# First projections of a hybrid trunk: groups of two, two, six and six k tiles, k tiles 2 to 5 modulated in pairs

## The chip, the cores and the metric

The kernel runs on one core of a Trainium2 chip. The metric is the time of one execution on the device in microseconds (us), as the median of the runs; less is better. The core has five engines that run side by side and meet by semaphores: TensorE (PE; its weight loads are shown as PEld), VectorE (DVE), ScalarE (ACT), GpSimd (POOL) and SyncE (SP), which here issues the transfers between HBM and the core's memory. Each engine takes its own list of instructions in order.

## The reference

One layer of a hybrid trunk, on x of 512 x 2048 and one conditioning vector c of 2048, all in float32. What matters here is its beginning:

```python
mod = c @ w_ada[l] + b_ada[l]
sh1, sc1, g1, sh2, sc2, g2 = [m[:, None, :] for m in jnp.split(mod, 6, axis=-1)]
h = x * (1.0 + sc1) + sh1
mix = token_mixer(h, ...)        # begins with proj = h @ w_in
x = layer_norm(ALPHA * x + g1 * mix, ln1_g[l], ln1_b[l])
h = x * (1.0 + sc2) + sh2
ff = jnp.square(jax.nn.relu(h @ w_ff1[l])) @ w_ff2[l]
x = layer_norm(ALPHA * x + g2 * ff, ln2_g[l], ln2_b[l])
```

`proj` is split into u, the convolution's inputs, q, k, v, and the indexer's qi, ki and wi. No column of `h` is known before its scale and shift are, and these need a product of c with 16 x 256 weights for each 128 columns.

## The kernel before

**Tiles.** The 2048 columns of `h` are 16 k tiles of 128. `acts` holds them transposed, 128 columns x 512 tokens, each as a high and a low half: `split(h, l, src)` has ACT round to fp32r (`wh` of a weight, L57) and DVE subtract (`wl` of a weight, L60). A product of two float32 numbers is three matmuls (`mm3`, `mm3n`): high x high, low x high, high x low.

**Modulation of w k tiles (`start_k`).** DVE accumulates c[i] times 16 blocks of w_ada into the tile `adaz` of 128 x 256w (`ada_acc`: one instruction a block on L63, the first of a tile on L67; loads `raw`, four buffers of 1 MB). PE adds up its 128 partitions against `ones` (L299, tile `sc`). DVE adds the bias and one (tile `mod`). Then, for each of the w k tiles, ACT forms `hf` = x * scale + shift (x comes as the tile `xk`), ACT rounds it into `acts`, and DVE subtracts for its low half. Two buffers each hold `adaz`, `xk` and `hf`.

**First projections.** u and kiwi (weights `wA` and `wkw`), then qi (`wqi`, two halves), then q (`wq`, two halves) are computed in four groups of k tiles, `KGROUPS`. A group does all five weight blocks for its k tiles. A k tile costs 15 matmuls for `wA` and `wkw`, 2 x 9 for `wqi` and 2 x 12 for `wq`: 57, nearly all with 512 columns. The weights of two k tiles come as one tile `rw`, and are split as one piece of 128 x 1024. At the end of a group its sums leave PSUM (`evac_acc`): by ACT in the first group, by DVE, which adds them to what is there (`u_t`, `qi_n`, `q_t`), in the others. Two banks of u and that of kiwi stay in PSUM through all groups.

**Order.** Work is written group by group; the accumulations for the next group's k tiles are written a step at a time between this group's weights (`pace`, `tick`), and `ensure(k1 - 1)` writes out what is still missing of a group's k tiles ahead of its first weights. A scheduler with priorities (`PRIO`) then sets the order on each engine; on the chip each engine follows that order. The groups are called 0 to 3 below.

Of the kernel before, what the change touches and what calls it, by code (L numbers as in the profile page):

```python
# [16 lines left out]
SEQ, D, NT, KT = 512, 2048, 4, 16  # L17
# [2 lines left out]
NH, HD = 8, 128  # L20
IH = 16
TOPK = 128
KGROUPS = ((0, 2), (2, 6), (6, 10), (10, 16))

PRIO = dict(cols=40000, ada_bias=4000, mod=4000, kw=4000, first=4000, evac=1000, values=300, att=600, mixer=150,
            wo=5000, ln1=150, ff1=3000, ff2=4000, hc=300, hc_load=300, tx=2000, ln2=150, index=-100, topk=60, rope=600, ssm0=600, ssm=300, glu=150,
# [25 lines left out]
def trunk_kernel(ctx, tc, A, out):  # L52
# [3 lines left out]
    def act(o, i, f=AF.Copy, **kw):  # L56
        S.activation(o, i, f, **kw)  # L57

    def tt(o, a, b, op):
        V.tensor_tensor(o, a, b, op=op)  # L60
# [4 lines left out]
    def ts(o, a, s1, s2, op0, op1=None):  # L65
        if op1 is None:
            V.tensor_scalar(o, a, s1, None, op0=op0)  # L67
        else:
            V.tensor_scalar(o, a, s1, s2, op0=op0, op1=op1)
# [11 lines left out]
    def prio(name):  # L81
        if name not in PRIO:
            name += str(stage_no[0])
        return tc.high_priority(offset=PRIO[name])

    def bank(n="mm"):
        if "two" in pools:
            return two_banks()[:, 0]
        return pools[n].tile([128, 512], F32, name=n)
# [9 lines left out]
    def col(n, i=0, w=1):  # L99
        o = COLS[n][0]  # L100
        return cols[:, o + i:o + i + w]
# [18 lines left out]
    def split(h, l, src):  # L120
        act(h, src)
        tt(l, src, h.bitcast(F32), OP.subtract)
# [92 lines left out]
    def ada_acc(srcs, n, brow=None, ways=1, pool=None):  # L215


        z = (pool or AZ[0]).tile([128, ways * n], F32, name="adaz", bufs=2 if pool else 1)
        if brow is not None:
            G.memset(z, 0.0)  # L220
            with prio("ada_bias"):
                nc.sync.dma_start(z[0:1, :], brow)
        i = 0
        for s in srcs:
            r = load(s, [128, s.shape[1], n], *ada_raw, prio_="ada_load")
            with prio("ada"):
                for j in range(s.shape[1]):
                    o = z[:, (i % ways) * n:(i % ways + 1) * n]
                    if i < ways and brow is None:
                        ts(o, r[:, j], col("c", i), None, OP.mult)  # L230
                    else:
                        stt(o, r[:, j], col("c", i), o, OP.mult, OP.add)
                    i += 1
            yield z

    def ada_block(blk, sink, row=False):
        src = [A["adaR"][blk][:, 2 * j:2 * j + 2] for j in range(8)]
        for z in ada_acc(src, 1024, A["bR"][blk:blk + 1, :] if row else None):
            yield
        sink(z)  # L240
# [9 lines left out]
    def to_cols(dst, bias):  # L250
        def sink(z):
            ps = bank("sc")
            for j in range(8):
                T.matmul(ps[:, j:j + 1], z[:, j * 128:(j + 1) * 128], ones[:, 0:1], start=True, stop=True)
            tt(dst, ps[:, 0:8], bias, OP.add)
        return sink
# [25 lines left out]
    def start_k(k, w):  # L282

        if w == 4:
            src = A["adaS4"][(k - 2) // 4]
        else:
            src = A["adaS2"][k // 14][:, :, 256 * (k % 2):256 * (k % 2 + w)]
        step = 8 // w
        ways = 2 if w == 1 else 1
        for i, z in enumerate(ada_acc([src[:, a:a + step] for a in range(0, 16, step)], 256 * w,  # L290
                                      ways=ways, pool=FP)):
            if i < 2 * w - 1:
                yield
        ps = bank("sc")
        mod = FP.tile([128, 2 * w], F32, name="mod")
        for j in range(2 * w):
            for a in range(ways):
                c0 = (a * 2 * w + j) * 128
                T.matmul(ps[:, j:j + 1], z[:, c0:c0 + 128], ones[:, 0:1], start=a == 0, stop=a == ways - 1)  # L299
        with prio("mod"):  # L300
            tt(mod, ps[:, 0:2 * w], col("bS", 2 * k, 2 * w), OP.add)
            sc_ = mod.rearrange("p (k two) -> p k two", two=2)[:, :, 0]
            ts(sc_, sc_, 1.0, None, OP.add)
            for j in range(w):
                xk = FP.tile([128, SEQ], F32, name="xk")
                nc.sync.dma_start(xk, A["xT"][k + j])
                hf = FP.tile([128, SEQ], F32, name="hf")
                act(hf, xk, AF.Identity, scale=mod[:, 2 * j:2 * j + 1], bias=mod[:, 2 * j + 1:2 * j + 2])
                split(acts[:, k + j, 0], acts[:, k + j, 1], hf)
        ready[0] = k + w  # L310
        yield

    def start_all():
        k = 0
        while k < KT:
            w = 1 if k < 2 else min(4, KT - k)
            yield from start_k(k, w)
            k += w

    bg.append(start_all())  # L320

    held = [bank("sa"), bank("sa"), bank("sb")]

    def ensure(k):
        while ready[0] <= k:
            tick()
# [4 lines left out]
    for j in range(2):  # L331
        mod_jobs.append(ada_block(2 + j, to_cols(mod2[:, 1, 8 * j:8 * j + 8], col("b2", 8 * j, 8))))
        mod_jobs.append(ada_block(4 + j, to_cols(mod2[:, 0, 8 * j:8 * j + 8], col("b2", 16 + 8 * j, 8))))
    for gi, (k0, k1) in enumerate(KGROUPS):
        n_ada = 2 * (KGROUPS[gi + 1][1] - KGROUPS[gi + 1][0]) if gi + 1 < len(KGROUPS) else PUMP["start"]
        n_w = 5 * (k1 - k0) - (k1 - k0 if gi == 0 else 0)
# [8 lines left out]
        if gi > 0:  # L345
            ensure(k1 - 1)
        if gi == len(KGROUPS) - 1:
            bg.extend(mod_jobs[:3])
# [686 lines left out]
    with prio("ln1"):  # L1035
        for t in range(NT):
# [3 lines left out]
            for kq in range(4):  # L1040
                ps = bank(("sa", "sb")[kq % 2])
                for j in range(4):
                    k = 4 * kq + j
                    T.transpose(ps[:, j * 128:(j + 1) * 128], r1[:, t, k * 128:(k + 1) * 128], ident)
                hf = WO.tile([128, 4, 128], F32, name="hf2", bufs=3)
                for j in range(4):
                    k = 4 * kq + j
# [582 lines left out]
```

## Time and profile before

| | |
|---|---|
| median of 3 runs | 2221.06 us (2219.15 to 2222.51) |
| the profiled execution | 2218.12 us |
| its span from first to last instruction | 2216.3 us |
| PE busy | 2138.7 us, 96% of the span |
| DVE busy | 1878.6 us, 85% |
| ACT busy | 1041.5 us, 47% |

The first projections are the first 250 us of the span. All rows are of the profiled execution; its span is 1.8 us shorter than its time. A busy PE is not always a PE at its peak: matmuls overlap each other, so that a wait of less than about 0.2 us between two of them does not show as idle time, and the distance from start to start is the better measure.

### The profile page before, as it was taken

What the parts mean: (1) busy time and instruction counts of PE and PEld (TensorE: products, weight loads), DVE (VectorE), ACT (ScalarE), POOL (GpSimd) and SP (SyncE); (2) the same over time, 40 slices, a digit from 0 to 9 for tenths busy, and PEclk for the clock granted to TensorE, in tenths of its full rate; (3) what the DMA queues carried; (4) which work ended last, traced back from release to release, by engine and by line L of the source; (5) the groups of instructions that cost most, each with busy time, mean ns of one, the idle gap of its engine ahead of it and who ended that gap; (6) DMA issues with size and microseconds to landing.
All of it is one profiled execution on the core that took longest, in us unless ns stands there. A gap on an engine that the chain in (4) does not pass through costs nothing.

```text
span 2216.3 us, 30985 instructions
## 1 busy us (share of the span) xinstructions
PE 2138.7 (96%) x12043; PEld 1845.9 (83%) x12043; DVE 1878.6 (85%) x2520; ACT 1041.5 (47%) x1394; POOL 44.6 (2%) x55
## 2 busy tenths in 40 slices
PE   6999999998999999989999999999899999999997
PEld 4778887876777787889999999999778887888886
DVE  7886799999867776798888888886789988998788
ACT  3423444344644313666666665665444444444432
POOL 0000000010000000000000000000000000000000
PEclk9999999999999999999999999999999999999999
DMA  8887653364334676756566556564888898798462
GB/s 326 316 305 280 200 216 135 107 235 164 103 119 157 243 277 255 241 172 229 182 205 203 188 198 206 181 209 141 301 295 275 280 318 280 245 341 275 134 218 86
DMA packets 198171, 489.80 MB, mean 221 GB/s; under 512 B 18052, under 2 KB 106500, under 8 KB 171656
## 3 DMA queue, kind: packets, MB, share of 16 engines
q1 hardware_dynamic: 191496, 475.24, 61.0%
q0 software_dynamic: 6528, 12.58, 3.1%
q8 instruction: 94, 1.54, 0.3%
q14 instruction: 53, 0.43, 0.1%
HBM read 394.45 MB, written 80.74 MB: 214 GB/s over the span
## 4 chain that ended last, share of the span: by engine, by line
PE 50%; issue 29%; DVE 14%; DMA 4%; ACT 3%; SPq 0%; POOL 0%; DVEq 0%; ACTq 0%; POOLq 0%
PE two L1396 7%; PE two L1397 7%; PE two L1395 7%; PE mm L209 4%; PE mm L197 4%; PE mm L210 4%; PE mm L208 3%; PE mm L198 3%; PE mm L196 3%; DVE wl L60 3%; DVE adaz L63 2%; PE two L210 1%; PE two L209 1%; PE two L208 1%; DVE x L60 1%
## 5 line engine op out<-in xcount | busy, mean ns | idle before, releaser
L57 ACT ACTIVATE wh<-raw 128x1024 fp32r<-128x1024 f32 x332 | 351.1, 1058 | 437.5 <-PE two L1397 140.8
L60 DVE TENSOR_TENSOR wl<-raw,wh 128x1024 fp32r<-128x1024 f32 x332 | 403.7, 1220 | 106.5 <-ACT wh L57 105.3
L1395 PE MATMUL two<-wh,hin 128*128 128x512 f32 x784 | 307.4, 392 | 5.7 <-ACT wh L57 5.0
L1396 PE MATMUL two<-wl,hin 128*128 128x512 f32 x784 | 306.5, 391 | 4.1 <-DVE wl L60 4.0
L1397 PE MATMUL two<-wh,hin 128*128 128x512 f32 x784 | 305.8, 390 | 0.0
L196 PE MATMUL mm<-acts,wh 128*128 128x512 f32 (+1 forms) x568 | 223.0, 396 | 5.7 <-ACT wh L57 3.3
L197 PE MATMUL mm<-acts,wl 128*128 128x512 f32 (+1 forms) x568 | 224.0, 394 | 1.7 <-DVE wl L60 1.5
L198 PE MATMUL mm<-acts,wh 128*128 128x512 f32 (+1 forms) x568 | 221.2, 391 | 0.0
L63 DVE SCALAR_TENSOR_TENSOR adaz<-raw,cols,adaz 128x1024 f32<-128x1024 f32 (+2 forms) x180 | 198.2, 1111 | 16.9 <-DMA raw<-in_adaR_dram 12.8
L202 PE MATMUL mm<-acts,wh 128*128 128x256 f32 x720 | 204.0, 283 | 3.1 <-ACT wh L57 2.4
L203 PE MATMUL mm<-acts,wl 128*128 128x256 f32 x720 | 203.8, 283 | 1.8 <-DVE wl L60 1.8
L203 PE MATMUL mm<-tx,wl 128*128 128x256 f32 x720 | 203.8, 283 | 1.1 <-DVE wl L60 1.1
L204 PE MATMUL mm<-acts,wh 128*128 128x256 f32 x720 | 203.7, 283 | 0.0
L204 PE MATMUL mm<-tx,wh 128*128 128x256 f32 x720 | 203.3, 282 | 0.0
L202 PE MATMUL mm<-tx,wh 128*128 128x256 f32 x720 | 202.0, 281 | 0.1
L1395 PEld LDWEIGHTS two<-wh,hin 128*128 128x128 f32 x784 | 147.7, 188 | 38.0 <-ACT wh L57 6.2
L1396 PEld LDWEIGHTS two<-wl,hin 128*128 128x128 f32 x784 | 147.6, 188 | 37.9 <-DVE wl L60 6.6
L209 PE MATMUL mm<-wl,acts 128*128 128x512 f32 x448 | 175.1, 391 | 1.7 <-DVE wl L60 1.5
L210 PE MATMUL mm<-wh,acts 128*128 128x512 f32 x448 | 174.5, 390 | 0.0
L208 PE MATMUL mm<-wh,acts 128*128 128x512 f32 x448 | 173.6, 391 | 0.2 <-DVE r L60 0.2
L1397 PEld LDWEIGHTS two<-wh,hin 128*128 128x128 f32 x784 | 147.6, 188 | 30.7
L57 ACT ACTIVATE wh<-st 128x1024 fp32r<-128x1024 f32 x90 | 95.5, 1061 | 105.3 <-PE mm L204 82.8
(316 smaller groups left out, 4514.5 us busy)
## 6 DMA issues: line engine op xcount, KB each, us to landing
raw<-in_wff_dram SPq DMA_DIRECT2D x232, 512.0 KB, 4.9
hc_d<-hc SPq DMA_DIRECT2D x98, 512.0 KB, 5.1
hin<-hc_d SPq DMA_DIRECT2D x49, 1024.0 KB, 9.2
raw<-in_adaR_dram SPq DMA_DIRECT2D x48, 1024.0 KB, 5.6
raw<-in_adaS_dram SPq DMA_DIRECT2D x32, 1024.0 KB, 9.0
raw<-in_wo_dram SPq DMA_DIRECT2D x16, 1024.0 KB, 5.3
araw<-in_adaR_dram SPq DMA_DIRECT2D x16, 1024.0 KB, 7.8
raw<-in_wconv_dram SPq DMA_DIRECT2D x12, 1024.0 KB, 5.0
```

The lines of the kernel that those rows point to most:

```text
L57: S.activation(o, i, f, **kw)
L60: V.tensor_tensor(o, a, b, op=op)
L196: T.matmul(ps, wh, xh, start=start, stop=False)
L197: T.matmul(ps, wl, xh, start=False, stop=False)
L198: T.matmul(ps, wh, xl, start=False, stop=stop)
L202: T.matmul(ps, wh, xh, start=start, stop=False, skip_group_check=True)
L203: T.matmul(ps, wl, xh, start=False, stop=False, skip_group_check=True)
L204: T.matmul(ps, wh, xl, start=False, stop=stop, skip_group_check=True)
L209: T.matmul(ps, xh, wl, start=False, stop=False)
L1395: T.matmul(ps[:, t], xh, h[:, k], start=first, stop=False, skip_group_check=True)
L1396: T.matmul(ps[:, t], xh, l[:, k], start=False, stop=False, skip_group_check=True)
L1397: T.matmul(ps[:, t], xl, h[:, k], start=False, stop=last, skip_group_check=True)
```

## The change

The four groups become k tiles 0-1, 2-3, 4-9 and 10-15, where they were 0-1, 2-5, 6-9 and 10-15. K tiles 2-3 and 4-5 are modulated as two pairs (w = 2), where they were one group of four (w = 4); k tiles 6-9 and 10-13 stay groups of four, 14-15 a pair. For a pair the source is half of each block of four in HBM, in runs of 2 KB.

```diff
-KGROUPS = ((0, 2), (2, 6), (6, 10), (10, 16))
+KGROUPS = ((0, 2), (2, 4), (4, 10), (10, 16))
...
         if w == 4:
             src = A["adaS4"][(k - 2) // 4]
+        elif 2 <= k < 14:
+            src = A["adaS4"][(k - 2) // 4][:, :, 512 * ((k - 2) % 4 // 2):][:, :, 0:512]
         else:
             src = A["adaS2"][k // 14][:, :, 256 * (k % 2):256 * (k % 2 + w)]
...
-            w = 1 if k < 2 else min(4, KT - k)
+            w = 1 if k < 2 else 2 if k < 6 else min(4, KT - k)
```

The scheduler's order differs between the two kernels on PE, DVE, ACT and SP up to the last group of the first projections, and is the same from there on. Three places follow. In all of them the number behind a name tells one tile from another.

On ACT, in group 0: `wh_345` of before and `wh_339` of the change are the high half of the first `wq` weights, `wh_427` and `wh_403` that of the second. Before:

```order
L57 ACTIVATE qi_n0_105<-mm_293 128x512
L57 ACTIVATE qi_n1_106<-mm_294 128x512
L57 ACTIVATE qi_n2_107<-mm_295 128x512
L57 ACTIVATE wh_345<-rw_335 128x1024
L57 ACTIVATE q_t0_117<-mm_331 128x512
L57 ACTIVATE q_t0_117<-mm_332 128x512
L57 ACTIVATE q_t0_117<-mm_333 128x512
L57 ACTIVATE q_t0_117<-mm_334 128x512
L57 ACTIVATE wh_427<-rw_381 128x1024
```

The change, where `hf_393` and `hf_399` are the modulated k tiles 2 and 3:

```order
L57 ACTIVATE wh_339<-rw_331 128x1024
L57 ACTIVATE qi_n0_105<-mm_291 128x512
L57 ACTIVATE qi_n1_106<-mm_292 128x512
L57 ACTIVATE qi_n2_107<-mm_293 128x512
L57 ACTIVATE wh_403<-rw_375 128x1024
L57 ACTIVATE q_t0_117<-mm_327 128x512
L57 ACTIVATE q_t0_117<-mm_328 128x512
L57 ACTIVATE q_t0_117<-mm_329 128x512
L57 ACTIVATE q_t0_117<-mm_330 128x512
L57 ACTIVATE hf_393<-xk_391,mod_384 128x512
```

The two high halves stand one block of evacuations earlier, and `hf` of k tiles 2 and 3 comes ahead of group 0's last evacuation; before, it stood behind it.

On PE, in the last `wq` block of group 0 (24 matmuls into `mm_377` to `mm_380` before, `mm_371` to `mm_374` in the change): the sums for the modulation of group 1's k tiles. Before:

```order
L196 MATMUL mm_380<-acts_91,wh_427 128x512
L197 MATMUL mm_380<-acts_91,wl_428 128x512
L198 MATMUL mm_380<-acts_91,wh_427 128x512
L299 MATMUL sc_391<-ones_83,adaz_259 128x1 x8
L196 MATMUL sa_122<-acts_91,wh_468 128x512
```

The change:

```order
L197 MATMUL mm_373<-acts_91,wl_404 128x512
L301 MATMUL sc_383<-ones_83,adaz_259 128x1 x4
L198 MATMUL mm_373<-acts_91,wh_403 128x512
L196 MATMUL mm_374<-acts_91,wh_403 128x512
L197 MATMUL mm_374<-acts_91,wl_404 128x512
L198 MATMUL mm_374<-acts_91,wh_403 128x512
```

Before, the sums stand behind all 24 matmuls of the block; in the change behind the first 8, with 16 more to follow.

On DVE, in group 1, in the middle of the accumulations for group 2's k tiles (`adaz_463` before, `adaz_537` in the change). Before, with the low halves of the second half of `wqi` and of the first of `wq` (`wl_664`, `wl_699`, `wl_733`):

```order
L63 SCALAR_TENSOR_TENSOR adaz_463<-raw_659,cols_76,adaz_463 128x1024
L60 TENSOR_TENSOR wl_664<-rw_657,wh_663 128x1024
L63 SCALAR_TENSOR_TENSOR adaz_463<-raw_694,cols_76,adaz_463 128x1024 x2
L60 TENSOR_TENSOR qi_n0_105<-mm_630,qi_n0_105 128x512
L60 TENSOR_TENSOR wl_699<-rw_692,wh_698 128x1024
L60 TENSOR_TENSOR qi_n1_106<-mm_631,qi_n1_106 128x512
L63 SCALAR_TENSOR_TENSOR adaz_463<-raw_728,cols_76,adaz_463 128x1024
L60 TENSOR_TENSOR qi_n2_107<-mm_632,qi_n2_107 128x512
L63 SCALAR_TENSOR_TENSOR adaz_463<-raw_728,cols_76,adaz_463 128x1024
L60 TENSOR_TENSOR wl_733<-rw_726,wh_732 128x1024
```

The change, from the evacuations of the second half of `wqi` to the low halves of the two `wq` blocks of k tiles 2 and 3 (`wl_624`, `wl_706`):

```order
L63 SCALAR_TENSOR_TENSOR adaz_537<-raw_572,cols_76,adaz_537 128x1024 x2
L60 TENSOR_TENSOR qi_n0_105<-mm_567,qi_n0_105 128x512
L63 SCALAR_TENSOR_TENSOR adaz_537<-raw_576,cols_76,adaz_537 128x1024
L60 TENSOR_TENSOR qi_n1_106<-mm_568,qi_n1_106 128x512
L63 SCALAR_TENSOR_TENSOR adaz_537<-raw_576,cols_76,adaz_537 128x1024
L60 TENSOR_TENSOR qi_n2_107<-mm_569,qi_n2_107 128x512
L63 SCALAR_TENSOR_TENSOR adaz_537<-raw_580,cols_76,adaz_537 128x1024 x2
L60 TENSOR_TENSOR wl_624<-rw_613,wh_623 128x1024
L63 SCALAR_TENSOR_TENSOR adaz_537<-raw_615,cols_76,adaz_537 128x1024 x2
L63 SCALAR_TENSOR_TENSOR adaz_537<-raw_619,cols_76,adaz_537 128x1024
L60 TENSOR_TENSOR q_t0_117<-mm_609,q_t0_117 128x512
L63 SCALAR_TENSOR_TENSOR adaz_537<-raw_619,cols_76,adaz_537 128x1024
```

Before, one or two accumulations stand between one low half of weights and the next; in the change six stand ahead of `wl_624`, and behind it `wl_706` follows only after four more.

## Rows read from the trace of the kernel before

**Rows 1.** The page, part 1: busy us, share, instructions of each engine.

```profile
PE 2138.7 (96%) x12043; PEld 1845.9 (83%) x12043; DVE 1878.6 (85%) x2520; ACT 1041.5 (47%) x1394; POOL 44.6 (2%) x55
```

**Rows 2.** Windows: stretch, its length, busy us and count by engine, clock, DMA.

```profile
40.00:60.00 20.00, 15.79 (x64) 12.50 (x63) 14.41 (x16) 10.06 (x16) 0.00 (x0) 0.85 0.54 203
57.80:103.30 45.50, 45.17 (x197) 35.98 (x197) 40.09 (x45) 13.96 (x19) 0.00 (x0) 0.97 0.91 350
103.30:171.60 68.30, 66.66 (x302) 53.84 (x303) 59.29 (x80) 24.18 (x34) 0.00 (x0) 1.00 0.77 284
172.00:240.00 68.00, 68.00 (x300) 55.37 (x300) 42.52 (x50) 23.12 (x29) 0.00 (x0) 1.00 0.74 255
```

**Rows 3.** Timeline, PE: start, us, instruction xcount, idle before and releaser.

```profile
38.20 1.21 PE L196 MATMUL mm<-acts,wh 128*128 128x512 f32 x4 [1.63 <-ACT wh L57]
...
45.92 1.21 PE L196 MATMUL mm<-acts,wh 128*128 128x512 f32 x4 [1.63 <-ACT wh L57]
...
48.20 0.63 PE L197 MATMUL mm<-acts,wl 128*128 128x512 f32 x1
...
48.62 0.63 PE L198 MATMUL mm<-acts,wh 128*128 128x512 f32 x1
...
53.43 1.84 PE L299 MATMUL sc<-ones,adaz 128*128 128x1 f32 x16
...
57.80 0.80 PE L196 MATMUL sa<-acts,wh 128*128 128x512 f32 x1 [2.53 <-ACT acts L57]
...
171.58 0.63 PE L196 MATMUL sa<-acts,wh 128*128 128x512 f32 x2
```

**Rows 4.** Timeline, ACT and DVE, of groups 0 and 1.

```profile
35.24 1.96 ACT L57 ACTIVATE qi_n<-mm 128x512 f32<-128x512 f32 x3 [2.12 <-PE mm L210]
37.09 1.05 ACT L57 ACTIVATE wh<-rw 128x1024 fp32r<-128x1024 f32 x1
...
55.71 1.52 ACT L57 ACTIVATE hf<-xk,mod 128x512 f32<-128x512 f32 x2 [0.54 <-DVE mod L67]
...
26.06 0.75 DVE L67 TENSOR_SCALAR adaz<-raw,cols 128x1024 f32<-128x1024 f32 x1
...
85.42 1.22 DVE L60 TENSOR_TENSOR wl<-rw,wh 128x1024 fp32r<-128x1024 f32 x1
86.56 2.60 DVE L63 SCALAR_TENSOR_TENSOR adaz<-raw,cols,adaz 128x1024 f32<-128x1024 f32 x2
```

**Rows 5.** Groups by form to 240 us, DVE: busy us, mean ns, idle before.

```profile
L63 DVE SCALAR_TENSOR_TENSOR adaz<-raw,cols,adaz 128x1024 f32<-128x1024 f32 x56 | 71.7, 1281 | 9.7 <-DMA raw<-in_adaR_dram 7.9 <-DMA raw<-in_adaS_dram 0.9
L60 DVE TENSOR_TENSOR wl<-rw,wh 128x1024 fp32r<-128x1024 f32 x39 | 47.6, 1220 | 11.6 <-ACT wh L57 11.6
...
L60 DVE TENSOR_TENSOR qi_n<-mm,qi_n 128x512 f32<-128x512 f32 x18 | 12.1, 685 | 1.1 <-PE mm L210 1.1
...
L63 DVE SCALAR_TENSOR_TENSOR adaz<-raw,cols,adaz 128x512 f32<-128x512 f32 x15 | 11.2, 746 | 1.1 <-DMA raw<-in_adaS_dram 0.9
L60 DVE TENSOR_TENSOR acts<-hf,acts 128x512 fp32r<-128x512 f32 x16 | 10.8, 686 | 2.6 <-ACT acts L57 2.5
```

**Rows 6.** The same for ACT.

```profile
L57 ACT ACTIVATE wh<-rw 128x1024 fp32r<-128x1024 f32 x39 | 41.3, 1059 | 89.2 <-DMA rw<-in_wqi_dram 23.4 <-PE mm L198 21.1 <-DMA rw<-in_wq_dram 20.2
L57 ACT ACTIVATE hf<-xk,mod 128x512 f32<-128x512 f32 x16 | 12.5, 812 | 24.4 <-DVE mod L67 19.8 <-DMA rw<-in_wqi_dram 2.9 <-DVE kwl L60 0.9
L57 ACT ACTIVATE acts<-hf 128x512 fp32r<-128x512 f32 x16 | 9.4, 620 | 0.1
```

**Rows 7.** Timeline, SP and ACT: x for k tiles 8 and 9.

```profile
104.89 1.03 SPq L306 DMA_DIRECT2D xk<-in_xT_dram  x2
...
107.55 0.82 ACT L57 ACTIVATE hf<-xk,mod 128x512 f32<-128x512 f32 x1
```

**Rows 8.** The page, part 6: a load of 512 KB, us from issue to landing.

```profile
raw<-in_wff_dram SPq DMA_DIRECT2D x232, 512.0 KB, 4.9
```

**Rows 9.** Timeline, PE: a wait behind the first projections.

```profile
505.49 0.63 PE L719 MATMUL sb<-ident,s 128*128 128x128 f32 x4 [2.65 <-DVE s L60]
```

## The prediction

> **What bounds the kernel now.** I read the shares of the engines first: PE is busy for 96% of the span, DVE for 85% [rows 1]. So what the change is worth must be read from PE's idle time in the first projections, and from how near DVE comes to it there. The windows give both [rows 2]. Between 172 and 240 us, in the last group, PE does 300 matmuls in 68.00 us, one in 0.227 us: that is its full pace, and a k tile of 57 matmuls costs 12.9 us. DVE is busy there for 42.52 of 68 us. But from 57.80 to 103.30 us, in group 1, DVE is busy for 40.09 of 45.5 us, 88%: it accumulates four k tiles for group 2 while PE works on four of its own.
>
> The timeline of PE shows what is lost ahead of that [rows 3]. Twice in group 0 PE waits 1.63 us for the high half of a `wq` block, at 38.20 and 45.92 us. ACT's timeline says why: it evacuates three banks of `qi_n` from 35.24 us, and only then, at 37.09 us, rounds the weights [rows 4]. At 53.43 us come the sums of the modulation for group 1, and 2.53 us after their end, at 57.80 us, the first matmul of group 1, which waited for `acts` [rows 3]; `hf` had begun at 55.71 us [rows 4]. Between 40 and 60 us the granted clock is 0.85 on average [rows 2]: some matmuls ran at 1.2 GHz, and stand 0.42 us apart (48.20 and 48.62 us) [rows 3]. Group 3 begins at 171.58 us [rows 3]. From there on both kernels have the same order on every engine, so the change is worth what it does to this time, if nothing behind takes it up.
>
> **The change, part by part.** *Group 0 is faster.* Its first `wq` matmul came at 38.20 us after a wait of 1.63 us [rows 3]; in the change the high half stands ahead of the evacuations of `qi_n`, so it comes at 36.6 us. 24 matmuls take 5.4 us, to 42.0; the next high half is early too, and 8 more matmuls end at 43.8 us. There stand the sums, four products in place of eight: half of 1.84 us [rows 3], to 44.8 us. Are they ready? DVE's queue for them begins at 26.06 us [rows 4] and holds 16 narrow accumulations at 0.746 us and three low halves at 1.220 us [rows 5]: 15.6 us, to 41.7, and about a microsecond of waits for ACT. They are. 16 matmuls still follow, to 48.4 us, and cover the way of the modulation: `hf` 0.44 us behind the end of the sums as before (55.27 to 55.71 us [rows 3, 4]), at 45.2 us, two `hf` of 0.81 us, two `acts` of 0.62 us [rows 6], one evacuation of some 0.65 us (three take 1.96 us [rows 4]), and then the high half of group 1's first weights, 1.06 us [rows 6]: 49.8 us. Group 1 begins there instead of at 57.80 us: 8.0 us gained, with a clock that has had no reason to fall.
>
> *Group 1 has half the cover.* Two k tiles are 114 matmuls, 25.9 us, where four were 51.8. In their shade DVE must make ready not four k tiles but six: 4 and 5 for group 2, and 6 to 9, since group 2 is now six k tiles long and PE has the sums of 6 to 9 in its list ahead of group 2's first matmul. DVE's list from the end of the first sums to the last accumulation of `adaz_537` holds 16 narrow accumulations (16 x 0.746 = 11.9), 16 wide ones (16 x 1.281 = 20.5), five low halves of weights (5 x 1.220 = 6.1), 13 evacuations (13 x 0.685 = 8.9) and four low halves of `acts` (4 x 0.686 = 2.7) [rows 5]; the first of a tile is a cheaper form, 0.75 us for a wide one [rows 4], which I let stand for the small work left out. Sum: 50.2 us. The list begins at 44.9 us, so it ends at 95.1. Neighbours that don't need each other overlap by 0.08 us (a low half at 85.42 of 1.22 us, the next at 86.56 [rows 4]), which takes off up to 3 us; DVE in turn waits some 3 us for ACT and PE. I take 95.5 us. In that time PE is done with its 114 matmuls and stands: at each block of weights it waits for a low half that DVE has behind accumulations, longest ahead of the first `wq` block of k tiles 2 and 3 (six wide ones there, 7.7 us), and at the end for the sums. These take 1.84 us [rows 3], and group 2 begins at 97.3 us. From 49.8 us that is 47.5 us for 25.9 us of matmuls and 2.8 us of sums: 18.8 us lost.
>
> The narrow form adds to it. Two narrow accumulations cost 1.492 us, a wide one 1.281 [rows 5]: 0.211 us for each extra instruction, 16 of them in the change, 8 of these in group 1's list (1.7 us, in the sum already). The Trainium skill, "VectorE: DVE Perf Modes", section on the fixed extra latency per instruction, says that an operation from SBUF pays a fixed cost, some 150 cycles at 0.96 GHz, or an estimated 0.16 us; by it the eight would cost 1.3 us, and the sum would be 0.4 us smaller. Its advice to use at least 512 elements is kept here, and the rows still show a price.
>
> *The seam inside group 2.* Group 2 begins with 30 matmuls for k tiles 4 and 5, 6.8 us, to 104.1 us. K tile 6 needs the way of the modulation again, and its weights. SP has the load of these behind the third and fourth `xk`, which wait for a free buffer, so for the first and second `hf`. Sums end 97.3; `hf` at 98.4 (one evacuation on DVE stands between); second `hf` done about 101.0; the load of the weights, 512 KB, is issued at 101.4 and lands after 4.9 us [rows 8], 106.3; high half 1.06 us: 107.4. PE waits 3.3 us. The same two buffers showed before: `xk` for k tiles 8 and 9 issued at 104.89 us, and `hf` 2.66 us later [rows 7]. From below the wait is nothing, if the weights are there and `hf` is quick; from above about 5 us, if the low half, 1.2 us more, binds as well. I take 3.3.
>
> *The rest of group 2.* Six k tiles are 342 matmuls, 77.6 us, and 2.8 us of sums. DVE has 67 us of work in that time by the same prices (15 low halves, 16 evacuations, 8 `acts`, 16 wide and 16 narrow accumulations), so PE is the bound on average. Before, the stretch from 103.30 to 171.60 us took 68.3 us [rows 2] for 276 matmuls (62.7) and 2.8 us of sums: 2.8 us of small waits. I put the same in.
>
> *Bytes.* The 4 MB for the two pairs move in runs of 2 KB. They are issued behind fewer loads than before, and the last is due at about 39 us; nothing in the list waits for them by more than the microsecond allowed above, so this costs nothing. If that cover failed, a few microseconds in group 0 would be lost.
>
> **The sum.** Group 3 begins at 97.3 + 3.3 + 77.6 + 2.8 + 2.8 = 183.8 us instead of 171.58: 12.2 us later. The profiled execution took 2218.12 us for a span of 2216.3, so it would take 2230.3. The median of the runs is 2.9 us above the profiled one, so the forecast for the median is 2233.3 us.
>
> **The rivals.** A change within 0.2%, 4.4 us, is about what a measurement of this kernel cannot tell from none.
>
> *A. The early start is kept (faster).* Group 1 begins 8.0 us early, and two waits at 1.2 GHz go with it. If PE met no new wait in group 1, group 3 would begin 8 to 10 us early: about 2212 us. For that DVE's list of 50.2 us would have to pass in 28.7 us; the point from which it decides is 38 us, where gain and loss are equal. The prices of rows 5 don't leave that open, and DVE was at 88% before with less to do for each k tile of cover. Chance 0.04.
>
> *B. Lost, and taken up later (same).* If work behind the first projections waits for something that is not late, it would give the 12 us back. PE's later waits, such as that at 505.49 us, are for DVE and ACT [rows 9], which feed on the first projections and are late as well; and between 172 and 240 us PE has no idle time to give. A smaller loss, within 4.4 us, would also come from the lowest ends of all terms: DVE done at 92, no seam, no small waits: 92 + 1.8 + 77.6 + 2.8 = 174.2 us, 2.6 us late, 2223.7. Chance 0.07.
>
> *C. More waits than I see (slower still).* After a long wait in group 1 the clock falls, as it did between 40 and 60 us; DVE's list in group 2, 67 of 86 us, comes in bursts; the seam takes its upper end. Two times 1.5 us for matmuls at 0.42 instead of 0.227 us, 2 us of seam, and 5 us of bursts (twice the small waits of before) make 22 us: 2243. What decides is whether a low half stands behind accumulations in group 2 as it does in group 1; the lists show one or two there. Chance 0.14.
>
> *The forecast*, 5 to 18 us slower: 0.75.
>
> **How the numbers follow.** Slower has 0.75 + 0.14 = 0.89, same 0.07, faster 0.04. The range leaves out A, most of B and the far part of C: 2225 (B's low terms with half the seam) to 2241 us (the forecast with both clock terms, the upper seam and half the bursts).
>
> **What would show it.** In the profile of the changed kernel: the two waits of 1.63 us gone; the first sums of four products at 44 us, group 1 from about 50; DVE over 90% busy from 50 to 95 us; PE waits named for DVE `wl` and for the sums with some 19 us together before 97 us, the longest ahead of a `wq` block; a wait near 104 us for ACT `wh` or `acts`; group 3 from 184 us; the same distances from there to the end. I am wrong if DVE's list ends well before 95 us, if the scheduler's order lets PE work on something else meanwhile (I found nothing in its list), or if the end of the span moves by less than the start of group 3.

## The result, and the profile after

The changed kernel takes 2238.07 us (median of 6 runs, 2228.48 to 2239.82) where the kernel before took 2220.82 in the same series: 1.0072 times, 95% interval 1.0054 to 1.0090. A second series of five runs gave 2236.14 against 2222.27, 1.0059 (1.0045 to 1.0073). It is slower, as forecast (2233.3, range 2225 to 2241). The profiled execution took 2239.82 us, its span 2238.1.

The windows of after, the same four stretches as [rows 2]:

```profile
40.00:60.00 20.00, 16.95 (x76) 12.77 (x75) 16.58 (x27) 8.72 (x16) 0.00 (x0) 1.00 0.91 336
57.80:103.30 45.50, 33.93 (x114) 25.41 (x115) 40.51 (x51) 9.54 (x14) 0.00 (x0) 0.79 0.69 258
103.30:171.60 68.30, 67.88 (x300) 54.18 (x299) 56.76 (x70) 23.75 (x33) 0.00 (x0) 0.99 0.84 315
172.00:240.00 68.00, 65.60 (x286) 53.08 (x285) 39.02 (x48) 18.89 (x24) 0.00 (x0) 0.97 0.71 243
```

The second row is the loss: 114 matmuls in 45.5 us instead of 197, DVE busy for 40.51 us as before (40.09), the granted clock 0.79 instead of 0.97, and the DMA engines busy for 0.69 instead of 0.91. The last row is a second, smaller one that was not forecast: 286 matmuls instead of 300 in group 3.

The timeline of PE of after, the rows that answer to [rows 3] and every wait of over 1 us from there to 240 us (line numbers from L288 on are two higher than before):

```profile
43.27 0.95 PE L301 MATMUL sc<-ones,adaz 128*128 128x1 f32 x8
...
48.70 0.73 PE L196 MATMUL sa<-acts,wh 128*128 128x512 f32 x2 [0.69 <-ACT wh L57]
...
59.23 0.50 PE L209 MATMUL mm<-wl,acts 128*128 128x512 f32 x1 [1.67 <-DVE wl L60]
...
67.51 1.22 PE L208 MATMUL mm<-wh,acts 128*128 128x512 f32 x2 [3.37 <-ACT wh L57]
...
69.36 0.63 PE L210 MATMUL mm<-wh,acts 128*128 128x512 f32 x1
69.79 0.63 PE L209 MATMUL mm<-wl,acts 128*128 128x512 f32 x1
...
77.77 0.50 PE L196 MATMUL mm<-acts,wh 128*128 128x512 f32 x1 [1.29 <-DVE qi_n L60]
...
81.42 0.80 PE L197 MATMUL mm<-acts,wl 128*128 128x512 f32 x1 [3.14 <-DVE wl L60]
...
96.85 2.66 PE L301 MATMUL sc<-ones,adaz 128*128 128x1 f32 x16 [1.42 <-DVE adaz L63]
99.37 1.20 PE L196 MATMUL sa<-acts,wh 128*128 128x512 f32 x2
...
102.08 0.63 PE L197 MATMUL sa<-acts,wl 128*128 128x512 f32 x1
102.50 0.63 PE L198 MATMUL sa<-acts,wh 128*128 128x512 f32 x1
...
183.99 0.39 PE L196 MATMUL sa<-acts,wh 128*128 128x512 f32 x1
...
220.99 0.80 PE L208 MATMUL mm<-wh,acts 128*128 128x512 f32 x1 [2.40 <-DVE qi_n L60]
```

The first sums come at 43.27 us, group 1 at 48.70 instead of 57.80, 9.1 us early. Then PE waits again and again, and runs at half clock behind the longer waits (69.36 and 69.79 us: 0.43 us apart). Group 2 begins at 99.37, at first at half clock too (102.08 and 102.50). Group 3 begins at 183.99 us instead of 171.58, 12.4 us late. The wait of 2.40 us at 220.99 had no counterpart before.

To follow the distance further I take one place that every profile has, a wait of PE for DVE's `rot` behind the first projections. It stood at 380.99 us before; called **the mark** below. Before, then after:

```profile
380.99 1.07 PE L479 MATMUL sa<-ident,rot 128*128 128x128 f32 x8 [0.21 <-DVE rot L60]
```

```profile
397.33 1.07 PE L481 MATMUL sa<-ident,rot 128*128 128x128 f32 x8 [0.21 <-DVE rot L60]
```

The distance is 16.34 us there: 12.4 up to group 3, and 4 inside it. The spans differ by 21.8, so 5.5 us came later still; the experiments show whose these are.

### The profile page after: what moved, and what is told of

It reads as the page before. It is cut to its first block, busy times and chain, and to the rows that moved or that the text cites. A ratio compares the mean times of both kernels' runs of the same rounds, so it can differ in the third digit from the quotient of the medians.

```text
span 2238.1 us, 31004 instructions
## 1 busy us (share of the span) xinstructions
PE 2150.4 (96%) x12043; PEld 1853.2 (83%) x12043; DVE 1882.1 (84%) x2538; ACT 1040.5 (46%) x1394; POOL 44.6 (2%) x55
## 4 chain that ended last, share of the span: by engine, by line
PE 40%; issue 30%; DVE 21%; DMA 6%; ACT 2%; SPq 0%; DVEq 0%; POOL 0%; ACTq 0%; POOLq 0%
DVE wl L60 5%; PE two L1398 4%; PE two L1399 4%; PE two L1397 4%; PE mm L209 3%; PE mm L210 3%; PE mm L208 3%; DVE adaz L63 3%; PE mm L197 3%; PE mm L198 3%; PE mm L196 3%; DVE s L60 2%; PE two L209 1%; PE two L208 1%; PE two L210 1%
```

## The experiments

All are compared with the kernel before, run on the same chip. "Group 2" is the start of its first matmul; the mark is given as its distance to 380.99 us.

| kernel | time, us (before there) | ratio, 95% interval | group 2, us | mark, us |
|---|---|---|---|---|
| the change | 2238.07 (2220.82) | 1.0072, 1.0054 to 1.0090 | 99.37 | +16.34 |
| again_after | 2236.14 (2222.27) | 1.0059, 1.0045 to 1.0073 | 100.26 | +15.73 |
| again_before | 2225.0 (2222.11) | one run | 115.76 | +1.65 |
| groups_only | 2247.73 (2222.11) | 1.0113, 1.0096 to 1.0131 | 115.12 | +24.62 |
| pairs_only | 2226.06 (2222.11) | 1.0012, 1.0003 to 1.0021 | 118.88 | +3.73 |
| no_load_wait | 2231.02 (2222.27) | 1.0043, 1.0030 to 1.0055 | 98.01 | +11.99 |
| half_6to9 | 2234.32 (2222.11) | 1.0050, 1.0035 to 1.0064 | 93.66 | +10.48 |
| few_6to9 | 2230.49 (2224.36) | 1.0027, 1.0016 to 1.0037 | 90.44 | +5.14 |
| few_4to9 | 2231.84 (2224.36) | 1.0033, 1.0019 to 1.0046 | 90.24 | +7.46 |
| neither_6to9 | 2220.96 (2223.91) | 0.9988, 0.9976 to 1.0000 | 86.06 | -5.12 |
| list_6to9 | 2252.76 (2223.91) | 1.0122, 1.0107 to 1.0137 | 76.70 | +26.94 |
| lazy | 2235.84 (2222.27) | 1.0058, 1.0046 to 1.0071 | 115.49 | +12.88 |

In again_before, pairs_only and lazy the groups are those of before, where group 2 began at 114.28 us; in list_6to9 group 2 begins ahead of the sums, as told below. The profiles differ by up to 2.6 us before group 1 already: the first sums stand at 45.60 us in again_after and 44.90 in neither_6to9, and at 43.0 to 43.5 in the other seven kernels that begin group 1 so early. Apart from again_before, the mark and the difference of the medians agree within 3.3 us in every row: the mark stands for the loss, and nothing behind 380 us gives it back.

### The two halves of the change

**groups_only** is the kernel before with the first line of the diff alone:

```diff
-KGROUPS = ((0, 2), (2, 6), (6, 10), (10, 16))
+KGROUPS = ((0, 2), (2, 4), (4, 10), (10, 16))
```

> Groups of two, two, six and six k tiles, but k tiles 2 to 5 modulated as one four, as before. Theory (DVE's list for the next group no longer fits under a group of two k tiles): group 1 starts near 57.8 us as before; 66 matmuls later, near 73 us, PE stands for the sums of k tiles 6 to 9 until about 86 us, since DVE has 20.5 us of wide accumulations, 3.7 us of low halves and some 6 us of evacuations and acts ahead of them; group 3 starts near 184 us, 12 us later than before, and the time is 10 to 15 us above before. Rival 1 (the narrow pairs and the seam behind them cost the time): within 3 us of before. Rival 2 (only the clock's drops cost it): 3 to 5 us above.

Measured: 25.6 us slower, twice what I expected. PE's waits ahead of group 1 and two later ones, from its timeline:

```profile
54.37 3.55 PE L299 MATMUL sc<-ones,adaz 128*128 128x1 f32 x16 [5.22 <-DVE adaz L63]
...
61.27 0.80 PE L196 MATMUL sa<-acts,wh 128*128 128x512 f32 x1 [3.35 <-ACT acts L57]
...
90.87 3.55 PE L299 MATMUL sc<-ones,adaz 128*128 128x1 f32 x16 [3.35 <-DVE adaz L63]
...
107.54 1.65 PE L196 MATMUL mm<-acts,wh 128*128 128x512 f32 x3 [6.00 <-ACT wh L57]
```

The whole four must be ready after group 0, so group 1 begins at 61.27 us, later than before, and still has only two k tiles of cover. The sums for k tiles 6 to 9, expected at 86 us, come at 90.87, and a wait of 6.00 us that I had not expected follows. By the mark, the pairs bring back 8 to 9 us of this loss.

**pairs_only** is the changed kernel with the groups of before.

> Groups of two, four, four and six as before, but k tiles 2 to 5 modulated as two pairs. Theory: group 1 keeps its cover of four k tiles, so the wait ahead of group 2 doesn't come back; 16 extra instructions cost DVE 3.4 us in group 0, and k tiles 2 and 3 are ready earlier: 4 us faster to 1 us slower than before. Rival 1 (the narrow pairs cost the time): 8 to 15 us slower.

Measured: 4.0 us slower, 3 us outside what I expected and short of the rival's 8. 16 extra instructions at 0.211 us [rows 5] make 3.4 us, about that size, but where they bind was not taken apart: both sums now stand ahead of group 1, which begins at 62.59 us instead of 57.80.

### Group 3

**no_load_wait** changes one source, in the job for block 2 of the next modulation:

```diff
+                    if const:
+                        o3 = o
+                        c3 = acts[:, 15].rearrange("p a n -> p (a n)").bitcast(F32)
...
+                            stt(o3, c3, col("c", i), o3, OP.mult, OP.add)
...
-        for z in ada_acc(src, 1024, A["bR"][blk:blk + 1, :] if row else None):
+        for z in ada_acc(src, 1024, A["bR"][blk:blk + 1, :] if row else None, const=blk == 2):
```

> The changed kernel, but the first job of the next stage's modulation accumulates from values that have long been on the chip instead of from the tile that its load brings; the load is still issued, so the bytes are the same, and the output is not the reference's. Theory: the 4 us that the change lost inside group 3 come from that job. One of its accumulations stands on DVE between two evacuations of `qi_n` and waits 2.67 us for its load; the bank of PE stays taken, PE waits 2.40 us and then runs 3.41 us at half clock, 1.6 us more. Without the wait for the load, the distance to before at 250 us falls from 16.4 us to 12 to 13 us, and the time by 3 to 4 us against the changed kernel, to about 1.0055 times before. Rival: DVE's evacuations are late in group 3 for another reason, namely the amount of work ahead of them; then the wait of PE near 218 us stays at 2 us or more, and the time stays within 1 us of the changed kernel's.

> The changed kernel once more, on the chip that runs the two others, so that they are compared with it under the same conditions. Expected: 1.006 to 1.009 times the kernel before, 2234 to 2240 us. In its profile the distance to the first profile of before should again be about 12 us at the start of group 3 and about 16 us at 250 us, with the 2.40 us wait for `qi_n` near 218 us, since both come from the order and not from chance. What the first profile of the change lost beyond that, some 5 us between 900 us and the end, should differ from one execution to the next: the second profile of the kernel before had itself grown by 6.8 us against its first, at about the same places. If the whole 21.7 us come back, at the same places, that part belongs to the change after all.

Why this job was suspected stands in DVE's timeline of after:

```profile
215.68 0.69 DVE L60 TENSOR_TENSOR qi_n<-mm,qi_n 128x512 f32<-128x512 f32 x1 [0.40 <-PE mm L210]
219.05 1.28 DVE L63 SCALAR_TENSOR_TENSOR adaz<-raw,cols,adaz 128x1024 f32<-128x1024 f32 x1 [2.67 <-DMA raw<-in_adaR_dram]
220.25 0.68 DVE L60 TENSOR_TENSOR qi_n<-mm,qi_n 128x512 f32<-128x512 f32 x1
```

The first of three banks is evacuated at 215.68 us, then DVE stands for 2.67 us at an accumulation whose load is not there, and the evacuation of the second bank, which PE wants, starts 4.6 us behind the first. The kernel before has the three in one piece there, and so has no_load_wait. DVE's timeline of before, then of no_load_wait:

```profile
204.06 1.88 DVE L60 TENSOR_TENSOR qi_n<-mm,qi_n 128x512 f32<-128x512 f32 x3
```

```profile
214.54 2.05 DVE L60 TENSOR_TENSOR qi_n<-mm,qi_n 128x512 f32<-128x512 f32 x3 [0.40 <-PE mm L210]
```

PE has no wait of over 0.25 us from 152 to 250 us in no_load_wait, and the distance to before grows by 0.7 us from the start of group 3 to the mark (11.27 to 11.99), where it grew by 3.9 and 2.4 us in the two profiles of the change. The time is 5.1 us below that of the changed kernel beside it (expected 3 to 4). The theory held, but the run took away two things: the accumulations wait for no load, and they no longer stand between the evacuations. The second profile of the change shows the same place with smaller waits: 1.01 us at 220.50 and 1.02 at 233.14, and a mark of +15.73.

### DVE's list in group 1

**half_6to9** leaves out every second accumulation for k tiles 6 to 9:

```diff
-                for j in range(s.shape[1]):
+                for j in range(0, s.shape[1], skip):
...
+                                      ways=ways, pool=FP, skip=2 if k == 6 else 1)):
```

> The changed kernel, with only 8 of the 16 accumulations for k tiles 6 to 9 (every second one is left out, so these k tiles are modulated with other values); all loads stay. Theory (DVE's list sets the start of group 2): the list is 8 x 1.28 = 10.2 us shorter, group 2 starts near 88 us instead of 98.7, and the time is 8 to 12 us below the changed kernel's, near that of before. Rival (loads or PE's order set it): group 2 starts within 2 us of where it did, and the time stays.

Measured: the sums came at 91.88 us instead of 96.85, and the mark fell by 5 to 6 us, about half of what I expected. The window from the first sums to these:

```profile
44.00:91.80 47.80, 35.73 (x138) 26.29 (x137) 38.48 (x54) 13.39 (x20) 0.00 (x0) 0.93 0.80 306
```

DVE now idled for 9 of 47.8 us, and PE's two longest waits, 3.47 and 3.67 us, were no shorter than in the change (3.37 and 3.14). So DVE's amount of work was not all that held PE. My guess was that the three engines hold each other through their orders, and the next two were to test it.

**few_6to9** leaves out all but the first two of these accumulations, **few_4to9** also all but the first four for k tiles 4 and 5; every load is still issued:

```diff
-                for j in range(s.shape[1]):
+                for j in range(s.shape[1] if i < only else 0):
...
+                                      ways=ways, pool=FP, only=1 if k == 6 else 99)):    # few_4to9: k in (4, 6)
```

> The changed kernel with 2 of the 16 accumulations for k tiles 6 to 9 (all loads still issued; the output is not the reference's). Half of them left out took 5 us off the start of group 2; this takes 14 of 16 off, some 18 us of DVE's list, so that DVE has about 30 us to do where PE has 26 us of matmuls. If DVE's list is what holds PE in group 1, as forecast, the sums ahead of group 2 come at 78 to 83 us, and group 3 some 14 us earlier than in the changed kernel. Theory after the half: below some 42 us of list the three engines hold each other in their orders (ACT has `hf` of k tile 4 ahead of the high half that PE wants, DVE evacuates banks that PE has just filled, PE at half clock after each wait); then the sums stay at 88 to 92 us, PE's wait of 3.4 us for ACT `wh` near 67 us stays, and the time is 2228 to 2234 us.

> As before this one, and of the accumulations for k tiles 4 and 5 only 4 of 16 are left as well (all loads still issued; the output is not the reference's): another 9 us off DVE's list, all of it ahead of 63 us. Theory: the wait of PE for ACT `wh` near 67 us comes from `hf` of k tile 4 standing ahead of it on ACT, and `hf` waits for sums that PE has in its own list behind the `wA` blocks; so sums and `hf` move up by at most 2 us, the wait stays at 2 us or more, and the sums ahead of group 2 come at 85 to 91 us. Rival: that wait is DVE's lateness passed on through the sums of k tiles 4 and 5; then it vanishes, and group 2 begins another 5 to 9 us earlier than with the k tiles 6 to 9 alone.

Measured: group 2 at 90.44 and 90.24 us. The scheduler had moved the sums up to 65 us, so they can't be compared. In few_6to9 these sums also cover the wait for ACT `wh` near 67 us: ACT begins that high half at 66.43 us, as in the change (66.42), but PE is at the sums until 69 us. So that wait's absence says nothing against the theory of the orders. In few_4to9 `hf` of k tile 4 moved up by 8.8 us, not by 2 at most, so that part of the theory fell; and the rival fell too, since 8 us less on DVE changed nothing.

What was left ahead of the first `wq` block, in few_6to9:

```profile
69.26 1.04 ACT L57 ACTIVATE wh<-rw 128x1024 fp32r<-128x1024 f32 x1
...
75.94 1.39 DVE L60 TENSOR_TENSOR qi_n<-mm,qi_n 128x512 f32<-128x512 f32 x2 [0.18 <-PE mm L210]
77.25 1.22 DVE L60 TENSOR_TENSOR wl<-rw,wh 128x1024 fp32r<-128x1024 f32 x1
...
78.52 0.50 PE L197 MATMUL mm<-acts,wl 128*128 128x512 f32 x1 [1.45 <-DVE wl L60]
```

The high half is done at 70.30 us. Its low half stands on DVE behind the evacuations of banks that PE has only just filled, comes 7 us later, and PE waits for it. The same order stands ahead of the second `wq` block (a wait of 0.63 us at 85.73) and inside group 2 (2.67 us at 93.72). ACT stands for loads in the same stretch:

```profile
76.89 1.06 ACT L57 ACTIVATE wh<-rw 128x1024 fp32r<-128x1024 f32 x1 [6.59 <-DMA rw<-in_wq_dram]
82.44 1.52 ACT L57 ACTIVATE hf<-xk,mod 128x512 f32<-128x512 f32 x2 [4.49 <-DMA xk<-in_xT_dram]
```

But the high half of 76.89 us is done at 77.95, and PE begins with it at 83.65. From 69 to 90 us no wait of PE ends with a load. The next two runs took ACT's waits for the cause all the same, and went after the bytes. The windows from 44 to 90 us, of few_6to9 and then of few_4to9:

```profile
44.00:90.00 46.00, 38.97 (x155) 29.54 (x156) 31.70 (x50) 15.83 (x24) 0.00 (x0) 0.89 0.93 354
```

```profile
44.00:90.00 46.00, 38.60 (x157) 29.60 (x157) 23.70 (x38) 15.86 (x24) 0.00 (x0) 0.89 0.94 364
```

DVE has gone from 31.70 to 23.70 us of work and group 2 did not move; the DMA engines are busy for 93 and 94% of the stretch.

### The bytes

**neither_6to9** leaves out 7 of the 8 loads of 1 MB as well, **list_6to9** keeps the accumulations and makes 14 of them from resident values:

```diff
 # neither_6to9
+            if i >= only:
+                yield z
+                continue
             r = load(s, [128, s.shape[1], n], *ada_raw, prio_="ada_load")
...
 # list_6to9
-            r = load(s, [128, s.shape[1], n], *ada_raw, prio_="ada_load")
+            r = load(...) if i < only else None      # then acts of k tile 0 in its place
```

> The changed kernel with only the first of eight loads for the modulation of k tiles 6 to 9, and only the 2 accumulations that use it (so neither the list of DVE nor 7 of the 8 MB are there; the output is not the reference's). With the accumulations left out and the bytes kept, group 2 still began only at 90.4 us, ACT waited 4.5 to 6.6 us at a time for loads of `wq` and `xk`, and 16.3 MB moved from 44 to 90 us with the DMA engines 93% busy. Theory: behind DVE's list stood the bytes; without them PE needs 26 us of matmuls and 3 us of sums from 48.7 us, and the first matmul of group 2 comes at 78 to 84 us, with ACT's waits for loads gone. Rival: the three engines hold each other by their orders whatever the loads do; then group 2 still begins at 87 to 91 us.

> The other half: the changed kernel with all 16 accumulations for k tiles 6 to 9 on DVE, but 14 of them made from values that are on the chip, and 7 of the 8 MB not loaded (the output is not the reference's). If DVE's list alone sets the end of group 1, as forecast, the first matmul of group 2 comes at 95 to 100 us as in the changed kernel (99.4), and the time stays within 3 us of its 2236 to 2238. If the bytes bind together with the list, at many places by turns, group 2 begins at 88 to 94 us.

neither_6to9: PE's timeline has no wait of over 0.25 us between 69 and 250 us. Group 2 begins at 86.06 us, between the two expectations, but group 1 began at 50.33, 1.6 us later than in few_6to9, and from 69 us PE did its work there at its pace. The mark moved by 10 us, from +5.14 to -5.12. Its window:

```profile
44.00:90.00 46.00, 41.18 (x185) 32.24 (x184) 39.82 (x62) 20.34 (x33) 0.00 (x0) 0.96 0.69 242
```

185 matmuls instead of 155, with the DMA engines at 69%. But the bytes are not all that changed. With the loads out of the way the scheduler gave another order, as SP's and DVE's timelines show:

```profile
54.47 0.97 SPq L127 DMA_DIRECT2D rw<-in_wq_dram  x2
...
71.33 1.23 DVE L60 TENSOR_TENSOR wl<-rw,wh 128x1024 fp32r<-128x1024 f32 x1
...
73.07 1.22 DVE L60 TENSOR_TENSOR wl<-rw,wh 128x1024 fp32r<-128x1024 f32 x1
74.20 0.69 DVE L60 TENSOR_TENSOR qi_n<-mm,qi_n 128x512 f32<-128x512 f32 x1
```

Both loads of `wq` are issued at 54 us, where few_6to9 has 63.39 and 66.47, and both low halves stand ahead of the evacuations behind which they stood there. So the 10 us belong to the bytes and to this order together, and no run here parts the two.

list_6to9: the sums came at 95.64 us, after a wait that PE's timeline shows in one piece:

```profile
95.64 3.54 PE L302 MATMUL sc<-ones,adaz 128*128 128x1 f32 x16 [15.21 <-DVE adaz L63]
```

DVE did not idle by more than 0.54 us at a time from 47 to 95 us: with 7 of the 8 MB gone, its list still holds PE up to the sums. It is no clean answer, though. Group 2 began at 76.70 us, ahead of the sums, and much of group 1's `wq` work went behind them (the first evacuation of `q_t` is at 109.10 us instead of 86.51), so the start of group 2 can't be held against the expectations. Six accumulations for k tiles 10 to 13 moved in among these as well (6.7 us), and the time was 28.9 us above before, instead of the change's 14 to 17.

### Early start with the old cover

**lazy** takes what I thought the lesson was, and tries to win:

```diff
-KGROUPS = ((0, 2), (2, 4), (4, 10), (10, 16))
+KGROUPS = ((0, 2), (2, 6), (6, 10), (10, 16))
...
+        n_ada = (4, 12, 12, PUMP["start"])[gi]
...
-            ensure(k1 - 1)
+            ensure(k0 + 1 if gi == 1 else k1 - 1)
...
+        def pace_a(n):           # for wA of group 1: its second pair writes out k tiles 4 and 5
+            pace(n)
+            seen[0] += n
+            ensure(seen[0] - 1)
```

> The groups of the kernel before (two, four, four and six k tiles), k tiles 2 to 5 in pairs as in the change, and one thing new: group 1 does not wait for the sums of all its four k tiles before its first matmul. It begins with k tiles 2 and 3, and the sums and the `acts` of 4 and 5 come in the program ahead of its second block of `wA`; in group 0 only the work for k tiles 2 and 3 is put in. Theory: the change lost its gain because the early group was also made a short one. The early start (8 us) can be kept and the cover of four k tiles too, so group 1 begins at about 49 us, PE waits 4 to 6 us for the sums of k tiles 4 and 5 between 57 and 62 us, group 1 ends 3 to 8 us earlier than before, and group 3 begins at 163 to 169 us instead of 171.58. The time is 2212 to 2219 us, 0.997 on average. Rival: DVE's list of modulation and weights sets the end of group 1 whatever PE does, as it was 88% busy there before; then the early start buys nothing, group 2 begins within 2 us of its old place, and the time is 2221 to 2228 us, as it was with the pairs alone (2226).

Measured: 13.6 us slower than before; the theory fell. PE's timeline:

```profile
48.65 0.73 PE L196 MATMUL sa<-acts,wh 128*128 128x512 f32 x2 [0.69 <-ACT wh L57]
...
61.32 1.84 PE L301 MATMUL sc<-ones,adaz 128*128 128x1 f32 x8 [5.43 <-DVE kwl L60]
65.69 0.80 PE L196 MATMUL sa<-acts,wh 128*128 128x512 f32 x1 [2.53 <-ACT acts L57]
...
153.57 1.65 PE L196 MATMUL mm<-acts,wh 128*128 128x512 f32 x3 [3.69 <-ACT wh L57]
```

The early start is there, and so is the wait of 5.43 us that I expected. What I had not counted is the way behind the sums (2.53 us) and 14 matmuls at half clock from 65.69 to 71.4 us, 0.43 us apart (2.8 us): with the sums themselves that is more than the 9 us gained, and group 2 begins at 115.49 us, as the rival had it (its time of 2221 to 2228 us was missed too). The rest is lost in group 2, first at 153.57 us, where the sums of the next four fell ahead of a `wq` block and ACT took `hf` before the block's `wh`. That is the order that came out, not a limit, and was not tried otherwise.

## Why the prediction was right, and where it was not

**Group 0 is faster: right.** Both waits of 1.63 us are gone; sums at 43.27 us (43.8 forecast), group 1 at 48.70 (49.8), the clock 1.00 from 40 to 60 us.

**Group 1 has half the cover: right in size and in cause, but not in what follows from less work.** The last accumulation of `adaz` ends at 96.7 us (95.5), the sums start at 96.85, and group 2 at 99.37 (97.3). The loss is 99.37 - 48.70 = 50.7 us for 25.9 us of matmuls and 3.7 of sums: 21.1 us, where I had 18.8. The waits that the timeline names make 12.4 of these, 26 matmuls at half clock 5. The longest waits were not where I put them: 3.37 us ahead of a `wqi` block, where ACT had just taken `hf` of k tile 4, and 3.14 ahead of the first `wq` block. The groups by form for DVE, from 44 to 97 us of after, bear out the list:

```profile
L63 DVE SCALAR_TENSOR_TENSOR adaz<-raw,cols,adaz 128x1024 f32<-128x1024 f32 x15 | 19.2, 1278 | 0.1
L63 DVE SCALAR_TENSOR_TENSOR adaz<-raw,cols,adaz 128x512 f32<-128x512 f32 x15 | 11.2, 748 | 0.3
L60 DVE TENSOR_TENSOR wl<-rw,wh 128x1024 fp32r<-128x1024 f32 x5 | 6.1, 1220 | 0.7 <-ACT wh L57 0.7
```

In the change DVE's list is the bound. The window of it, and the longest of SP's waits from 48.7 to 90 us (us in total, times, longest):

```profile
44.20:96.70 52.50, 39.47 (x139) 28.22 (x138) 47.38 (x61) 13.40 (x20) 0.00 (x0) 0.87 0.80 298
...
SPq L127 <- DVE adaz L63: 35.3, 9, 8.1
```

DVE is busy for 47.38 of 52.50 us, and the loads wait for DVE to free a buffer, not DVE for the loads. But rival A was said to decide at 38 us of list, and that is wrong: at 31.70 us of DVE work in few_6to9 the early start was still not kept. The step that failed there set the length of DVE's list against PE's time, and left out where the low halves stand in it: behind evacuations of banks that PE has just filled, they came late at 31.70 us of work, and at 23.70 us in few_4to9 just as late (a wait of 1.45 us at the first `wq` block in both).

*"Bytes ... costs nothing"* is about the four MB of the pairs, and for these it held: the first sums came at 43.27 us. The bytes of group 1 I passed over, though a row that I quoted had the DMA engines busy for 0.91 there [rows 2]. In the change they were at 0.69 in the same stretch, and DVE's accumulations of that window waited for none of them by more than 0.4 us in all (the last figures of the first two lines above), so the bytes did not bind. Of the loss in group 1, DVE's accumulations hold the first 9 us (99.37 to 90.44). Another 10 us, by the mark, went when the loads of k tiles 6 to 9 went too and the low halves came ahead of the evacuations; which of the two it was stays open.

**The narrow form** came out at 748 against 1278 ns, or 0.218 us for each extra instruction; the estimate of 0.16 us from the Trainium skill, "VectorE: DVE Perf Modes", section on the fixed extra latency, is the smaller one again, and the measurement stands.

**The seam inside group 2: not seen.** There is no wait near 104 us. In its place PE runs 8 matmuls at half clock from 101.22 us. (Two other profiles of the same groups show a small wait for ACT `wh` somewhat later: 0.54 us at 109.52 in again_after, 0.69 at 107.41 in no_load_wait.) Group 2 took 84.6 us from its start to group 3, 1.9 less than forecast; together with the start of group 2, 2.1 us later than forecast, the sum came out at 183.99 us (183.8). That two terms cancel here is luck.

**"From there on both kernels have the same order on every engine": wrong; the like sentence in the section on the change can hold only behind group 3.** The orders differ inside group 3, as the evacuations of `qi_n` show, and the step cost 3.9 us in the first profile, 2.4 in the second: the forecast of 2230.3 us for a profiled execution lacks them, and the difference of the medians, 17.3 and 13.9 us, lies on either side of the mark's 16.

**The last 5.5 us of the first profile are not shown to be the change's.** The kernel before, profiled again, had a mark of +1.65 and a span 6.9 us longer than its own first one, so it too lost 5.2 us behind the mark. The second profile of the change lost 5.1 there (20.8 - 15.7), no_load_wait 0.2. What sets this apart between executions stays open.

**The rivals.** A and B did not come; of C, the half clock came (26 matmuls in two stretches ahead of 90 us, 8 more in group 2) without the rest.

## What to carry to other kernels

An early start is worth only what the work behind it has ready: shortening a stage of PE shortens the time that the vector engine has for the next stage's work, so set that work against the new length, and look where in its list the pieces stand that PE wants first. When one limit has been found, take it away in an experiment before pricing the gain, for a second may stand a few microseconds beneath it. Leaving work out lets the scheduler order the rest anew: read the new order before calling the difference the price of what was left out. An engine that waits is a cause only if PE's own wait ends with it. And "the same order from here on" must be read from the instruction lists of both kernels as far as the claim reaches.

## What the runs showed of the hardware

Behind waits of 3.37 and 3.14 us PE ran 12 and 14 matmuls 0.43 us apart, the 1.2 GHz level, and 7 behind the 2.40 us at 220.99 us, which cost 1.4 to 2.8 us on top of the wait. That price is not fixed. Behind the same wait of 3.14 us the second profile had only some 8; and behind waits of 2.67 us (few_6to9, at 93.72), 2.02 us (few_4to9, at 212.12) and 1.01 and 1.02 us (the second profile, group 3) all but the first matmul kept the full pace of 0.23.

With the DMA engines 93 to 94% busy the core moved 354 to 364 GB/s for 46 us in loads of mostly 0.25 to 1 MB. The Trainium skill, "DMA: Bandwidth & Descriptors", section "Measured", has 341 GB/s for a transfer of 1 MB and 425 for one of 16 MB, issued from GpSimd, on a core alone; these runs lie near the first, and none here held the second over such a stretch. How long a load of `wq` takes does not follow from the share alone. The DMA view from 44 to 90 us, of after (share 0.86), few_6to9 (0.93) and before (0.81), the last number being the median in us from issue to landing:

```profile
rw<-in_wq_dram SPq DMA_DIRECT2D x2, 512.0 KB, 5.8
...
rw<-in_wq_dram SPq DMA_DIRECT2D x2, 512.0 KB, 10.3
...
rw<-in_wq_dram SPq DMA_DIRECT2D x4, 512.0 KB, 10.4
```

The kernel before differed by 5.2 us between its two profiled executions behind 380 us, and by 1.65 us ahead of it. A change of this size needs the median and the place where its distance arises, not one span.
